# A float32 encoder trunk on one core: every operand of a matrix product begins at a multiple of 256 bytes

## The chip, the cores and the metric

The kernel runs on one core of one Trainium2 chip. The metric is the device time of one execution in microseconds (us). Before the change the median of three runs is 2270.95 us (2270.53 to 2271.29).

## The reference, cut to what matters

The reference computes a trunk of two layers over 256 tokens of width 2048, in float32. Layer 0 is a combined input projection, a bidirectional mLSTM of 4 heads and an RG-LRU block next to each other, and an output projection. Layer 1 is dilated attention of 16 heads. Each layer ends in a SwiGLU feed-forward block, and a last RMS norm stands at the end. The part of layer 0 that the change touches, and the feed-forward block in which most of the products lie:

```python
hm = bidirectional_mlstm(qh, kh, vh, gates)
hm = hm * lax.rsqrt(jnp.mean(jnp.square(hm), axis=-1, keepdims=True) + RMS_EPS)
hm = jnp.transpose(hm, (0, 2, 1, 3)).reshape(B, S, MLSTM_WIDTH) * head_g.astype(jnp.float32)
y_a = hm * jax.nn.sigmoid(o.astype(jnp.float32))
y = jnp.concatenate([y_a, y_b], axis=-1).astype(h.dtype)
return y @ w_out

def swiglu(h, w1, w3, w2):
    return (jax.nn.silu(h @ w1) * (h @ w3)) @ w2
```

## The kernel before, in words

**Products.** The kernel gets near float32 accuracy out of the fp32r type by splitting each operand into a high part (the value cast to fp32r) and a low part (the rest). A product is then three matrix products: high by high, high by low and low by high. Weights come from HBM in units of 1 MB, `raw`, of 4 blocks of 128 rows by 512 columns. `emit_split` turns half a unit at a time into `wh` (line 204, ScalarE) and `wl` (line 205, VectorE). The four `raw` buffers are loaded over SP's queue, a new one as soon as the last half of an old one is split; splits are made three steps ahead of the products (`AHEAD`).

**Two forms.** A step is one half unit. In the narrow form (`narrow`, lines 272 to 274) the activations are the stationary operand, 128 tokens at a time, and 512 weight columns move: the sums have tokens on the partitions. This form serves the value and output gates of layer 0, the attention's values, all up and down projections of the feed-forward blocks and both output projections. A step has 12 products (2 blocks of rows, 2 halves of the tokens, 3 products), a unit 24. In the wide form (lines 294 and 295) 128x128 weights are stationary and the activations move, 512 columns (high and low part of all tokens) with `wh`, then 256 with `wl`. It serves the projections whose results are wanted with features on the partitions.

**Order.** `emit_step` writes out, step by step, the splits that come next, the products of the step and then one turn of the open tasks (`run_tasks`), which are generators: evacuations of finished sums, and the recurrent parts and attention heads, of which up to three are open at once. Each engine works through its own part of this order; `flags` hold a product's instructions back until its activations have been written out.

**Where things lie.** Tiles come out of pools, and the pools stand in SBUF one behind the other, in the order in which they are opened: `const`, `rawp`, `whp`, `wlp`, `evp`, `s8p`, `m4p`, `rbp`, `smp`. Inside a pool the tiles (or the buffers of one tag) follow each other in the order of their first use, each rounded up to 32 bytes for a partition. The build places the first tile of `const` at byte 16512 of each partition. In `const` lie the constants `cpk` (gains, biases and the like, a column for each block of 128 features), `cst` (identity and two triangles), `ehr`, `gbias`, `ones`, `half`, `hgh` and then `xT`, the activations of the layer as [128, 16 blocks, high and low, 256 tokens]; small tiles of 1216 bytes in all come behind. `s8p` has eight slots of `SLOT` values each, which hold among others `hT` (the activations of the down projections), `oT` (of the attention's output projection) and `ya`/`yb` (of layer 0's output projection). `m4p` has five tiles.

**The head gain.** `more_consts` loads `head_g` into `hgh`, [128, 1024], the same row on each partition, with a DMA from POOL's queue, and halves it (line 1016). `o_chunk` computes the tanh of the gate sums (line 790) and, on line 795, (tanh + 1) times `hgh` into `go`. `ml_out` multiplies the normed heads by `go` (line 760), transposes 128x128 blocks into PSUM, and writes the high part (line 773, ScalarE, two blocks at a time) and the low part (line 774, VectorE) into `ya`.

Of the kernel before, what the change touches and what calls it, by code (L numbers as in the profile page):

```python
# [9 lines left out]
F32 = mybir.dt.float32  # L10
F32R = mybir.dt.float32r
AF = mybir.ActivationFunctionType
ALU = mybir.AluOpType
# [4 lines left out]
P = 128  # L18
KB = D // P
CW = 512  # L20
# [4 lines left out]
RB = 8  # L25
# [5 lines left out]

G_E, G_F0, G_O, G_F1 = 0, 16, 32, 48
C_W, C_B = 64, 96
C_BA, C_BX, C_LAM = 104, 120, 136
C_N = 152


RAW_BUFS = 4
# [1 line left out]
AHEAD = 3  # L40

SLOTS = 8
SLOT = 2064
EV_BUFS = 6
M4_BUFS = 5

# [18 lines left out]
def trunk_kernel(ctx: ExitStack, tc: tile.TileContext, a, out):  # L65
    nc = tc.nc
    V, A, PE, GP, SP = nc.vector, nc.scalar, nc.tensor, nc.gpsimd, nc.sync

    const = ctx.enter_context(tc.tile_pool(name="const", bufs=1))
# [5 lines left out]
    m4p = ctx.enter_context(tc.tile_pool(name="m4p", bufs=M4_BUFS))  # L75
# [7 lines left out]
    def slot(shape, dt=F32, name="s8"):  # L83
        t = s8p.tile([P, SLOT], dt, tag="s8", name=name)
        n = int(np.prod(shape))
        v = t[:, :n]
        if len(shape) == 1:
            return v
        pat = {2: "p (a b) -> p a b", 3: "p (a b c) -> p a b c", 4: "p (a b c d) -> p a b c d"}[len(shape)]
        return v.rearrange(pat, **dict(zip("abcd"[1:], shape[1:])))  # L90

    def m4(shape, name="m4", dt=F32):
        t = m4p.tile([P, 1040], dt, tag="m4", name=name)
        n = int(np.prod(shape))
        return t[:, :n].rearrange("p (a b) -> p a b", b=shape[1])

    def ev(name="ev"):
        return evp.tile([P, CW], F32, tag="ev", name=name)

    def tp(name="tp"):  # L100
        return tpp.tile([P, 2, 256], F32, tag="tp", name=name)
# [6 lines left out]
    def lag():  # L108

        for _ in range(LAG):  # L110
            yield
# [10 lines left out]
    def sm(n, name="sm"):  # L122
        t = smp.tile([P, 32], F32, tag="sm", name=name)
        return t[:, :n]

    def bcast(ap_dram, n):
        return bass.AP(tensor=ap_dram.tensor, offset=ap_dram.offset, ap=[[0, P], [1, n]])


    cpk = const.tile([P, C_N], F32, name="cpk")  # L130
    cst = const.tile([P, 3, P], F32, name="cst")
    ehr = const.tile([MH, MH, P], F32R, name="ehr")
    gbias = const.tile([P, 16], F32, name="gbias")
    ident, upper, lower = cst[:, 0, :], cst[:, 1, :], cst[:, 2, :]
    ones = const.tile([P, P], F32, name="ones")
    half = const.tile([P, 16], F32, name="half")
    hgh = const.tile([P, 1024], F32, name="hgh")
    xT = const.tile([P, KB, 2, S], F32R, name="xT")

    def transpose(o, i, n=P):  # L140
        PE.transpose(o, i, ident[:n, :n])  # L141

    def power(dst, src, n):
        GP.tensor_tensor(dst, src, half[:, :n], op=ALU.pow)
# [34 lines left out]
    pos = {"load": 0, "split": 0}  # L179
# [336 lines left out]
    ml, ys = {}, {}  # L516
# [228 lines left out]
    def ml_out(c):  # L745
        while not {f"mh{2 * c}", f"mh{2 * c + 1}", f"go{c}"} <= flags:
            yield
        rs = sm(4, "mrs").rearrange("p (a b) -> p a b", a=2)
        V.tensor_scalar(rs, ml["ss"][:, :, 2 * c:2 * c + 2], 1.0 / DV, EPS, op0=ALU.mult, op1=ALU.add)
        rsf = rs.rearrange("p a b -> p (a b)")  # L750
        power(rsf, rsf, 4)
        yield
        yt = slot((4, 2, S), F32R, name="ya")
        ys["y", 4 * c] = yt
        es = []
        for t in range(2):
            y = ev("ya")
            for k in range(2):
                h = 2 * c + k
                V.scalar_tensor_tensor(  # L760
                    y[:, k * DV:(k + 1) * DV], ml["h"][:, t, h, :], rs[:, t, k:k + 1],
                    ml["go"][:, t, h * DV:(h + 1) * DV], op0=ALU.mult, op1=ALU.mult,
                )
            es.append(y)
        yield
        yield from lag()
        for p in range(2):
            ps = tp("yT")
            for k in range(2):
                for t in range(2):  # L770
                    f0 = (2 * p + k) * P
                    transpose(ps[:, k, t * P:(t + 1) * P], es[t][:, f0:f0 + P])
            A.copy(yt[:, 2 * p:2 * p + 2, 0, :], ps)
            V.tensor_tensor(
                yt[:, 2 * p:2 * p + 2, 1, :], ps, yt[:, 2 * p:2 * p + 2, 0, :].bitcast(F32), op=ALU.subtract
            )
            for k in range(2):
                flags.add(f"y{4 * c + 2 * p + k}")
            yield

    def o_chunk(c):
        def gen(ch):
            if c == 0:
                ml["go"] = slot((2, 1024), name="go")
                ml["ro"] = const.tile([P, 2], F32, name="ro")
                V.tensor_scalar(ml["ro"], cur["rstd"], 0.5, None, op0=ALU.mult)
            es = []
            for t in range(2):
                e = ev("oe")
                A.activation(e, ch.acc[t], AF.Tanh, scale=ml["ro"][:, t:t + 1])  # L790
                es.append(e)
            ch.acc = None
            yield
            for t in range(2):
                V.scalar_tensor_tensor(
                    ml["go"][:, t, c * CW:(c + 1) * CW], es[t], 1.0, hgh[:, c * CW:(c + 1) * CW],
                    op0=ALU.add, op1=ALU.mult,
                )
            flags.add(f"go{c}")
            yield  # L800

        return gen
# [203 lines left out]
    def more_consts():  # L1006
        GP.dma_start(cst, a["cst"])
        GP.dma_start(gbias, bcast(a["gate_b"], 16))
        ehot = ev("ehot")[:MH, :]
        GP.dma_start(ehot, a["ehot"].rearrange("p a b -> p (a b)"))  # L1010
        while pos["split"] < 16:
            yield
        GP.dma_start(hgh, bcast(a["head_g"], 1024))
        while pos["split"] < 24:
            yield
        V.tensor_scalar(hgh, hgh, 0.5, None, op0=ALU.mult)
        A.copy(ehr.rearrange("p a b -> p (a b)"), ehot)

    def first_rstd():
# [96 lines left out]
    ch = steps[-1]["ch"]  # L1116
# [23 lines left out]
def tiled(w):  # L1140

    k, n = w.shape
    return np.ascontiguousarray(w.reshape(k // 512, 4, P, n // CW, CW).transpose(3, 0, 2, 1, 4))


def blocks(w):

    n = w.shape[1]
    return np.ascontiguousarray(w.reshape(KB, P, n // P, P).transpose(2, 1, 0, 3)).reshape(n // P, P, 4, CW)


def per_partition(v):
    return v.reshape(-1, P).T
# [17 lines left out]
def arrange(x, e_norm, e_w_in, e_gate_b, e_conv_w, e_conv_b, e_rg_wa, e_rg_ba, e_rg_wx, e_rg_bx,  # L1171
            e_rg_lam, e_head_g, e_w_out, o_norm, o_w_qkv, o_w_o, f_norm, f_w1, f_w3, f_w2, final_norm):
    c = np.ascontiguousarray
    w = e_w_in[0]
    q, k, v, o, g, xr, gr = np.split(w, np.cumsum([512, 512, 1024, 1024, 16, 1024])[:6], axis=1)
    perm = np.r_[0:4, 8:12, 4:8, 12:16]
    cst, ehot, ab = constants()
    cpk = np.concatenate(
        [per_partition(e_norm[0]), per_partition(f_norm[0]), per_partition(o_norm[0]), per_partition(f_norm[1]),
         e_conv_w[0].reshape(4, RB, P).transpose(2, 1, 0).reshape(P, 32), per_partition(e_conv_b[0]),  # L1180
         per_partition(e_rg_ba[0].reshape(-1)), per_partition(e_rg_bx[0].reshape(-1)),
         per_partition(e_rg_lam[0].reshape(-1))], axis=1)
    rgw = np.stack([e_rg_wa[0], e_rg_wx[0]]).reshape(2, 2, RB // 2, 2, P, P)
    return {
        "xT": c(x[0].T.reshape(KB, P, S).transpose(1, 0, 2)),
        "x": c(x[0].reshape(2, P, D).transpose(1, 0, 2)),
        "w_v": tiled(v), "w_xr": blocks(xr), "w_qk": blocks(np.concatenate([q, k], axis=1)),
        "w_og": tiled(o), "w_gr": blocks(gr),
        "wg": c(g[:, perm].reshape(KB, P, 16).transpose(1, 0, 2)),
        "gate_b": c(e_gate_b[0][perm]),  # L1190
        "head_g": c(e_head_g[0]),
        "cpk": c(cpk), "cst": cst, "ehot": ehot, "abias": ab,
        "rgw": c(rgw.transpose(2, 4, 0, 1, 3, 5)).reshape(RB // 2, P, 8, P),
        "w_out": tiled(e_w_out[0]),
        "w_av": tiled(o_w_qkv[0][:, 2 * D:]), "w_aqk": blocks(o_w_qkv[0][:, :2 * D]),
        "w_o": tiled(o_w_o[0]),
        "w1": np.stack([tiled(f_w1[l]) for l in range(2)]),
        "w3": np.stack([tiled(f_w3[l]) for l in range(2)]),
        "w2": np.stack([tiled(f_w2[l]) for l in range(2)]),
        "final_norm": c(final_norm),  # L1200
    }
# [17 lines left out]
```

## Time and profile before

| | |
|---|---|
| median of three runs | 2270.95 us |
| the profiled execution | 2270.73 us |
| its span, first to last instruction | 2269.0 us |
| TensorE busy | 2251.6 us, 99% |
| VectorE busy | 1248.0 us, 55% |
| ScalarE busy | 1042.9 us, 46% |
| granted TensorE clock | 0.999 |
| read from HBM | 414.09 MB, 183 GB/s over the span |

An instruction's row names its source line, engine, operation, the tiles that it writes and reads, shapes and count. Busy time of TensorE counts each product from its start to its modelled end; products are pipelined, so one begins before the last has ended, and the mean duration of a product is longer than the distance from its start to the next one's. That distance is read from the timeline, which lists instructions in order with start and duration.

### The profile page before, as it was taken

The page shows a single profiled execution, that of the slowest core. Times are in us where ns is not written, and L with a number is a line of the kernel's source. Part 1 is how long each engine was busy: PE and PEld are TensorE (multiplying, and loading weights), DVE is VectorE, ACT ScalarE, POOL GpSimd, SP SyncE. Part 2 cuts the span into 40 slices and gives each one's busy share as a digit, 9 for nine tenths or more (in the row PEclk, how much of TensorE's full clock was granted, in tenths as well). Part 3 has the DMA queues.
Part 4 walks back from the last instruction along what each step waited for, and adds up shares of the span by engine and source line. Part 5 has one row for each costly group of instructions (what it writes and reads, how often), then busy time and mean ns, then how long its engine had stood idle before and what let it go on. Part 6 is the DMA issues. An engine that isn't in the chain of part 4 may idle for free.

```text
span 2269.0 us, 25922 instructions
## 1 busy us (share of the span) xinstructions
PE 2251.6 (99%) x10420; PEld 1846.6 (81%) x10420; DVE 1248.0 (55%) x1514; ACT 1042.9 (46%) x1339; POOL 23.8 (1%) x42
## 2 busy tenths in 40 slices
PE   9999999999999999999999999999999999999998
PEld 7878888888888888888888888888888888888886
DVE  6867755445444444455566666554455444444554
ACT  5667544444443344444454554454444433444443
POOL 1000000000000000000000000000000000000000
PEclk9999999999999999999999999999999999999999
DMA  7534645555555555555555555555555556555553
GB/s 287 185 121 149 223 167 193 185 184 184 184 186 193 194 186 186 185 185 171 191 191 177 178 182 176 176 179 185 185 185 183 186 190 217 181 187 186 184 190 112
DMA packets 61336, 417.86 MB, mean 184 GB/s; under 512 B 6972, under 2 KB 7628, under 8 KB 12448
## 3 DMA queue, kind: packets, MB, share of 16 engines
q1 hardware_dynamic: 58176, 406.35, 52.7%
q0 software_dynamic: 2608, 9.26, 1.2%
q8 instruction: 81, 1.33, 0.2%
q10 hardware_dynamic: 432, 0.60, 0.1%
q14 instruction: 39, 0.32, 0.0%
HBM read 414.09 MB, written 2.10 MB: 183 GB/s over the span
## 4 chain that ended last, share of the span: by engine, by line
PE 95%; DVE 2%; ACT 1%; issue 1%; DMA 1%; POOL 0%; POOLq 0%; DVEq 0%; SPq 0%; ACTq 0%
PE acc L272 26%; PE acc L273 26%; PE acc L274 26%; PE acc L294 8%; PE acc L295 4%; PE hTp L141 1%; DVE wl L205 1%; PE rgp L455 1%; ACT wh L204 1%; DMA raw<-in_w_v 1%; PE nT L141 0%; DVE xc L422 0%; PE apT L141 0%; PE num L725 0%; PE asc L863 0%
## 5 line engine op out<-in xcount | busy, mean ns | idle before, releaser
L205 DVE TENSOR_TENSOR wl<-raw,wh 128x1024 fp32r<-128x1024 f32 (+1 forms) x770 | 940.3, 1222 | 876.4 <-ACT wh L204 874.3
L204 ACT CAST wh<-raw 128x1024 fp32r<-128x1024 f32 (+1 forms) x770 | 804.3, 1046 | 905.3 <-PE acc L274 828.1
L272 PE MATMUL acc<-wh,xT 128*128 128x512 f32 x1664 | 663.8, 399 | 0.9 <-ACT wh L204 0.8
L273 PE MATMUL acc<-wl,xT 128*128 128x512 f32 x1664 | 657.5, 395 | 1.2 <-DVE wl L205 1.2
L274 PE MATMUL acc<-wh,xT 128*128 128x512 f32 x1664 | 657.2, 395 | 0.0
L274 PEld LDWEIGHTS acc<-wh,xT 128*128 128x128 f32 x1664 | 312.4, 188 | 75.9
L272 PEld LDWEIGHTS acc<-wh,xT 128*128 128x128 f32 x1664 | 312.4, 188 | 75.7 <-ACT wh L204 2.0
L273 PEld LDWEIGHTS acc<-wl,xT 128*128 128x128 f32 x1664 | 312.5, 188 | 74.7 <-DVE wl L205 2.2
L294 PE MATMUL acc<-xT,wh 128*128 128x512 f32 x896 | 322.0, 400 | 0.4 <-ACT v L663 0.4
L272 PE MATMUL acc<-wh,hT 128*128 128x512 f32 x704 | 277.4, 394 | 0.0
L273 PE MATMUL acc<-wl,hT 128*128 128x512 f32 x704 | 275.9, 392 | 0.0
L274 PE MATMUL acc<-wh,hT 128*128 128x512 f32 x704 | 275.8, 392 | 0.0
L295 PE MATMUL acc<-xT,wl 128*128 128x256 f32 x896 | 252.2, 281 | 0.0
L294 PEld LDWEIGHTS acc<-xT,wh 128*128 128x128 f32 x896 | 168.5, 188 | 38.9 <-ACT v L663 0.5
L295 PEld LDWEIGHTS acc<-xT,wl 128*128 128x128 f32 x896 | 168.2, 188 | 0.9 <-DVE wl L205 0.3
L274 PEld LDWEIGHTS acc<-wh,hT 128*128 128x128 f32 x704 | 132.2, 188 | 29.8
L272 PEld LDWEIGHTS acc<-wh,hT 128*128 128x128 f32 x704 | 132.3, 188 | 28.8
L273 PEld LDWEIGHTS acc<-wl,hT 128*128 128x128 f32 x704 | 132.4, 188 | 28.6
L963 ACT CAST hT<-hTp 128x512 fp32r<-128x512 f32 x44 | 25.8, 587 | 85.2 <-PE hTp L141 85.2
L964 DVE TENSOR_TENSOR hT<-hTp,hT 128x512 fp32r<-128x512 f32 x44 | 30.4, 691 | 57.1 <-ACT hT L963 57.1
L272 PE MATMUL acc<-wh,oT 128*128 128x512 f32 x128 | 51.0, 398 | 0.0
L274 PE MATMUL acc<-wh,oT 128*128 128x512 f32 x128 | 50.3, 393 | 0.0
(226 smaller groups left out, 1209.9 us busy)
## 6 DMA issues: line engine op xcount, KB each, us to landing
raw<-in_w SPq DMA_DIRECT2D x264, 1024.0 KB, 4.9
raw<-in_w_aqk SPq DMA_DIRECT2D x32, 1024.0 KB, 4.9
raw<-in_w_out SPq DMA_DIRECT2D x16, 1024.0 KB, 4.9
raw<-in_w_av SPq DMA_DIRECT2D x16, 1024.0 KB, 4.8
raw<-in_w_o SPq DMA_DIRECT2D x16, 1024.0 KB, 4.9
raw<-in_w_xr SPq DMA_DIRECT2D x8, 1024.0 KB, 8.6
raw<-in_w_qk SPq DMA_DIRECT2D x8, 1024.0 KB, 4.9
raw<-in_w_og SPq DMA_DIRECT2D x8, 1024.0 KB, 4.9
```

Source lines behind the costliest of these rows:

```text
L141: PE.transpose(o, i, ident[:n, :n])
L204: A.copy(hi[:, k], raw[:, k])
L205: V.tensor_tensor(lo[:, k], raw[:, k], hi[:, k].bitcast(F32), op=ALU.subtract)
L272: PE.matmul(acc, xh, hi[:, j, :], start=f, stop=False)
L273: PE.matmul(acc, xh, lo[:, j, :], start=False, stop=False)
L274: PE.matmul(acc, xl, hi[:, j, :], start=False, stop=e)
L294: PE.matmul(acc, wh[:, j, :], x2.rearrange("p a b -> p (a b)"), start=f, stop=False)
L295: PE.matmul(acc[:, :S], wl[:, j, :], x2[:, 0, :], start=False, stop=e)
L455: PE.matmul(ps[:, k * S:(k + 1) * S], wt[:, k, d, b, :], xc[:, b, :], start=True, stop=True)
L963: A.copy(h[:, 2 * p:2 * p + 2, 0, :], ps)
L964: V.tensor_tensor(h[:, 2 * p:2 * p + 2, 1, :], ps, h[:, 2 * p:2 * p + 2, 0, :].bitcast(F32), op=ALU.subtract)
```

## The change: places and sizes in SBUF, and the head gain on the other side of the transposition

The constants are put into another order, `cpk` is rounded up to 192 columns and gets the head gains as eight more columns, a slot grows from 2064 to 2112 values and an m4 tile from 1040 to 1088. `hgh` becomes eight columns, a gain for each partition, halved from `cpk`; its broadcast from HBM is gone. The gate `go` is only tanh + 1, written in place. The gain is multiplied in when `ya` is written, block by block, with the scalar operand of each partition. The arithmetic of the products and their order stay as they are.

```diff
@@ constants of the file
-C_BA, C_BX, C_LAM = 104, 120, 136
-C_N = 152
+C_BA, C_BX, C_LAM, C_HG = 104, 120, 136, 152
+C_N = 160
-SLOT = 2064
+SLOT = 2112
@@ m4
-        t = m4p.tile([P, 1040], dt, tag="m4", name=name)
+        t = m4p.tile([P, 1088], dt, tag="m4", name=name)
@@ trunk_kernel, the constants
-    cpk = const.tile([P, C_N], F32, name="cpk")
+    gbias = const.tile([P, 16], F32, name="gbias")
+    half = const.tile([P, 16], F32, name="half")
+    cpk = const.tile([P, 192], F32, name="cpk")[:, :C_N]
     cst = const.tile([P, 3, P], F32, name="cst")
     ehr = const.tile([MH, MH, P], F32R, name="ehr")
-    gbias = const.tile([P, 16], F32, name="gbias")
     ident, upper, lower = cst[:, 0, :], cst[:, 1, :], cst[:, 2, :]
     ones = const.tile([P, P], F32, name="ones")
-    half = const.tile([P, 16], F32, name="half")
-    hgh = const.tile([P, 1024], F32, name="hgh")
     xT = const.tile([P, KB, 2, S], F32R, name="xT")
+    hgh = const.tile([P, 16], F32, name="hgh")[:, :RB]
@@ ml_out
-            A.copy(yt[:, 2 * p:2 * p + 2, 0, :], ps)
-            V.tensor_tensor(
-                yt[:, 2 * p:2 * p + 2, 1, :], ps, yt[:, 2 * p:2 * p + 2, 0, :].bitcast(F32), op=ALU.subtract
-            )
             for k in range(2):
+                kb = 2 * p + k
+                g = hgh[:, 4 * c + kb:4 * c + kb + 1]
+                A.mul(yt[:, kb, 0, :], ps[:, k, :], g)
+                V.scalar_tensor_tensor(
+                    yt[:, kb, 1, :], ps[:, k, :], g, yt[:, kb, 0, :].bitcast(F32), op0=ALU.mult, op1=ALU.subtract
+                )
                 flags.add(f"y{4 * c + 2 * p + k}")
@@ o_chunk
-            es = []
+            go = ml["go"][:, :, c * CW:(c + 1) * CW]
             for t in range(2):
-                e = ev("oe")
-                A.activation(e, ch.acc[t], AF.Tanh, scale=ml["ro"][:, t:t + 1])
-                es.append(e)
+                A.activation(go[:, t, :], ch.acc[t], AF.Tanh, scale=ml["ro"][:, t:t + 1])
             ch.acc = None
             yield
-            for t in range(2):
-                V.scalar_tensor_tensor(
-                    ml["go"][:, t, c * CW:(c + 1) * CW], es[t], 1.0, hgh[:, c * CW:(c + 1) * CW],
-                    op0=ALU.add, op1=ALU.mult,
-                )
+            V.tensor_scalar(go, go, 1.0, None, op0=ALU.add)
@@ more_consts
-        while pos["split"] < 16:
-            yield
-        GP.dma_start(hgh, bcast(a["head_g"], 1024))
         while pos["split"] < 24:
             yield
-        V.tensor_scalar(hgh, hgh, 0.5, None, op0=ALU.mult)
+        V.tensor_scalar(hgh, cpk[:, C_HG:C_HG + RB], 0.5, None, op0=ALU.mult)
@@ arrange: the head gains become columns of cpk
-         per_partition(e_rg_lam[0].reshape(-1))], axis=1)
+         per_partition(e_rg_lam[0].reshape(-1)), per_partition(e_head_g[0])], axis=1)
-        "head_g": c(e_head_g[0]),
```

## The prediction

> **What bounds the kernel now.** I read the page first, its busy shares and its chain.
>
> ```profile
> span 2269.0 us, 25922 instructions
> PE 2251.6 (99%) x10420; PEld 1846.6 (81%) x10420; DVE 1248.0 (55%) x1514; ACT 1042.9 (46%) x1339; POOL 23.8 (1%) x42
> PE 95%; DVE 2%; ACT 1%; issue 1%; DMA 1%; POOL 0%; POOLq 0%; DVEq 0%; SPq 0%; ACTq 0%
> PE acc L272 26%; PE acc L273 26%; PE acc L274 26%; PE acc L294 8%; PE acc L295 4%; PE hTp L141 1%; DVE wl L205 1%; PE rgp L455 1%; ACT wh L204 1%; DMA raw<-in_w_v 1%; PE nT L141 0%; DVE xc L422 0%; PE apT L141 0%; PE num L725 0%; PE asc L863 0%
> ```
>
> TensorE is busy 99% of the span and holds 95% of the chain, 90% of it in the five product lines 272 to 274, 294 and 295. So the time is their number times the distance from one start to the next (the pitch). The groups by shape give the numbers:
>
> ```profile
> L272 PE MATMUL acc<-wh,xT 128*128 128x512 f32 x1664 | 663.8, 399 | 0.9 <-ACT wh L204 0.8
> L294 PE MATMUL acc<-xT,wh 128*128 128x512 f32 x896 | 322.0, 400 | 0.4 <-ACT v L663 0.4
> L272 PE MATMUL acc<-wh,hT 128*128 128x512 f32 x704 | 277.4, 394 | 0.0
> L272 PE MATMUL acc<-wh,oT 128*128 128x512 f32 x128 | 51.0, 398 | 0.0
> L272 PE MATMUL acc<-wh,ya 128*128 128x512 f32 x64 | 25.7, 401 | 0.0
> L272 PE MATMUL acc<-wh,yb 128*128 128x512 f32 x64 | 25.2, 394 | 0.0
> ```
>
> Lines 273 and 274 have the same counts as 272, line 295 that of 294. So there are 3 x 2624 = 7872 products of 512 columns with tokens stationary (4992 with xT, 2112 with hT, 384 each with oT and y), and 896 pairs on lines 294 and 295. The mean of 399 ns is a duration that overlaps the next product; the pitch comes from the timeline.
>
> Next I set pitch against address. The build of the kernel before puts the const pool at byte 16512 = 64 x 256 + 128. By the tiles' sizes xT then begins 96 bytes past a multiple of 256, and wh and wl (the moving operand of lines 272 to 274) 32 past one. The eight slots of 8256 bytes that hold hT, oT and y begin 32, 96, 160, 224 and again 32, 96, 160, 224 past one. Call d the stationary operand's start less the moving one's, modulo 256: xT has d = 64, the slots have 0, 64, 128, 192. Steps on t, j or kb are multiples of 512 bytes and leave d alone. The second layer's down projection goes through all four, and its timeline (start, length, line) shows where one slot gives way to the next:
>
> ```profile
> 1817.43 0.39 PE L272 MATMUL acc<-wh,hT 128*128 128x512 f32 x1
> ...
> 1828.34 0.40 PE L272 MATMUL acc<-wh,hT 128*128 128x512 f32 x1
> ...
> 1833.92 0.39 PE L272 MATMUL acc<-wh,hT 128*128 128x512 f32 x1
> ...
> 1839.42 0.39 PE L272 MATMUL acc<-wh,hT 128*128 128x512 f32 x1
> ...
> 1845.01 0.39 PE L272 MATMUL acc<-wh,hT 128*128 128x512 f32 x1
> ```
>
> The first stretch is 48 products with d = 0: 10.91 us / 48 = 227.3 ns. The next three are 24 products each: d = 128, 5.58 / 24 = 232.5 ns; d = 192, 5.50 / 24 = 229.2; d = 64, 5.59 / 24 = 232.9. Same instruction, same wh and wl, one neighbourhood: the address alone moves the pitch by 2.5%. For xT, d = 64, one up-projection stretch:
>
> ```profile
> 431.90 0.48 PE L272 MATMUL acc<-wh,xT 128*128 128x512 f32 x1
> ...
> 473.98 0.49 PE L141 MATMUL hTp<-cst,up 128*128 128x128 f32 x3
> L272 PE MATMUL acc<-wh,xT 128*128 128x512 f32 x60 | 23.8, 397 | 0.0
> ```
>
> That is 180 products (60 on each line) in 42.08 us, 233.8 ns with a longer first one (0.48 against 0.39), so 233.3 as the steady value: the d = 64 value of hT again.
>
> **The change part by part.** *Addresses.* gbias and half (64 bytes each) now stand first: 16512 + 128 = 65 x 256. cpk takes 768 bytes, cst 1536, ehr 2048, ones 512, so xT begins at 21504 = 84 x 256. Behind it the shrunken hgh (64) and the small tiles (1216, as before) make 1280 = 5 x 256; raw, wh, wl and ev are multiples of 256; slots are 8448 = 33 x 256 and m4 tiles 4352 = 17 x 256. So every d becomes 0 and every start 0. That this happens I take as worked out.
>
> d = 0 is measured, but only with both operands 32 past a multiple of 256; nothing in this trace begins at 0. I price at the d = 0 row, 227.3. The bounds: above, nothing gained (pitches as now); below, the pitch of a pass without the extra time, from these pieces of the chain of waits:
>
> ```profile
> 181.12 0.86 PE qkp L682 x4
> 1125.66 0.87 PE nT L141 x8
> ```
>
> Four passes of plain float32, which take 512 columns' time each, cost 0.86 / 4 = 215 ns, and eight 128-column transpositions 0.87 / 8 = 109 ns. Products of lines 272 to 274 have 12 ns above that even at d = 0.
>
> [...]
>
> The terms for the narrow products, the units of 24 counted by the slots the build hands out (hT: 32 units at d = 0, 32 at 192, 16 at 64, 8 at 128; oT 4 at 0, 8 at 192, 4 at 64; y 4 each):
> - xT: 4992 x (233.3 - 227.3) = 30.0 us.
> - d = 64: 576 x 5.6 = 3.2 us. d = 128: 288 x 5.2 = 1.5 us. d = 192: 1056 x 1.9 = 2.0 us. d = 0: 960, nothing.
>
> *The wide pairs* (moving xT, stationary wh or wl, d = 192). A run of 56 pairs in the attention, then the scores behind it:
>
> ```profile
> 1146.42 0.40 PE L294 MATMUL acc<-xT,wh 128*128 128x512 f32 x1
> ...
> 1165.97 0.28 PE L862 MATMUL asc<-aqk 128*128 128x256 f32 x1
> ...
> 1166.68 0.39 PE L294 MATMUL acc<-xT,wh 128*128 128x512 f32 x1
> L294 PE MATMUL acc<-xT,wh 128*128 128x512 f32 x56 | 19.6, 393 | 0.0
> ```
>
> 19.55 / 56 = 349 ns a pair. The scores are six 256-column products whose two operands lie in one tile, d = 0, and take 0.71 / 6 = 118 ns each. So a pair at d = 0 is 227.3 + 118 = 345 ns: 896 x 4 = 3.6 us. Bounds: 0, and down to 215 + 109 = 324, 896 x 25 = 22.4 us.
>
> *The gate of the heads.* The gain moves from o_chunk (line 795) to the transposed side (lines 773 and 774), cut in two for a gain per partition.
>
> ```profile
> L371 ACT ACTIVATE xT<-nT,cpk 128x256 fp32r<-128x256 f32 x48 | 22.4, 473 | 29.1 <-DVE xT L372 16.4 <-PE nT L141 12.7
> L773 ACT CAST ya<-yT 128x512 fp32r<-128x512 f32 x4 | 2.3, 578 | 2.9 <-PE yT L141 2.9
> L372 DVE SCALAR_TENSOR_TENSOR xT<-nT,cpk,xT 128x256 fp32r<-128x256 f32 x48 | 22.9, 483 | 13.3 <-ACT xT L371 13.0
> L774 DVE TENSOR_TENSOR ya<-yT,ya 128x512 fp32r<-128x512 f32 x4 | 2.7, 686 | 1.9 <-ACT ya L773 1.9
> L795 DVE SCALAR_TENSOR_TENSOR go<-oe,hgh 128x512 f32<-128x512 f32 x4 | 2.6, 684 | 0.0
> L1016 DVE TENSOR_SCALAR hgh<-hgh 128x1024 f32<-128x1024 f32 x1 | 0.7, 683 | 0.0
> ```
>
> Lines 371 and 372 are the very forms that lines 773 and 774 become. ScalarE: eight of 473 for four of 578, +1.5 us. VectorE: eight of 483 for four of 686, +1.1; two additions of 128x1024 at 683 (line 1016's form) for four of 684, -1.4; hgh's own scaling shrinks by up to 0.7. Where it falls:
>
> ```profile
> 200.00:300.00 100.00, 99.98 (x501) 83.70 (x500) 72.22 (x116) 57.97 (x83) 3.49 (x4) 1.00 0.55 190
> L274 PE MATMUL acc<-wh,ya x64: 388/393/401, 282.6 to 362.9; 128*128 128x512 f32 x64
> L774 DVE TENSOR_TENSOR ya<-yT,ya x4: 682/686/691, 230.0 to 269.4; 128x512 fp32r<-128x512 f32 x4
> ```
>
> TensorE is full there (99.98 of 100), VectorE (72) and ScalarE (58) have room, and y is done at 270 us while its first product starts at 282. What queues behind the added pieces are weight splits, made three steps ahead. I count 0; uncovered it costs at most 1.5 us. The broadcast of head_g leaves POOL's queue and the DMA engines (line 1013, 128 x 1024 x 4 bytes); between -0.5 and 0, I take 0. cpk's rows grow from 608 to 640 bytes, and the first product waits for raw weights, not for cpk: 0. Transpositions and small float32 products already sit at 109 and 215 ns: 0.
>
> *Sum.* 30.0 + 3.2 + 1.5 + 2.0 + 3.6 = 40.3 us. A part of it lies before 200 us, where gaps for ScalarE and VectorE will give some back; I take off 1 us. The profiled execution took 2270.73 us (2269.0 span and 1.7 around it), and the median is 2270.95. 2270.7 - 39.3 = 2231 us, its own range 2222 to 2250 (pitches of 226 to 230 throughout).
>
> **The rivals.** *Start zero removes the extra time too.* Only distance was seen, never a start at 0. If 32 past a line costs both readers something, the narrow pitch goes from 227.3 towards 215 and the pair from 345 towards 324: 7872 x 12.3 + 896 x 21 = 116 us more, 2115 us; half of it gives 2173. For it: plain float32 passes reach 215 with a weight load each. Against: they stream at half the rate, and the scores at d = 0 give 118, not 109. [...]
>
> *The stationary operand's own start decides, and 0 is bad.* The moving operand never varies on lines 272 to 274, so d and the stationary start can't be told apart there. With starts at 32, 96, 160 and 224 giving 227.3, 232.9, 232.5 and 229.2, the neighbours of 0 are the two good ones, and their mean, 228.3, would give 7872 x 1.0 = 8 us less gain, 2239. But if reads that all begin on the same boundary meet more often, every narrow product could cost what xT's costs now, 233.3: the d = 0 products lose 960 x 6.0, d = 192 1056 x 4.1, d = 64 and 128 0.4 and 0.8 each, +10.6 us, 2281. The place is the down and output projections. It decides from a common pitch of (4992 x 233.3 + 576 x 232.9 + 288 x 232.5 + 1056 x 229.2 + 960 x 227.3) / 7872 = 232.0 ns upward.
>
> *Nothing changes.* The pitch would belong to the slot's use and not to its address: 2270.7. Against it, xT and the hT slot with d = 64 agree to 0.4 ns in different stages.
>
> **How the numbers follow.** Forecast (2222 to 2250) 0.64; start zero pays too (2115 to 2222) 0.18; a smaller gain (2250 to 2266) 0.05; no change 0.05; the bad start (2275 and up) 0.08. A measurement of this kernel can tell about 0.2%, 4.5 us, from no change. So faster is 0.64 + 0.18 + 0.05 = 0.87, same 0.05, slower 0.08. The range 2170 to 2262 holds the forecast, most of the smaller gain and about half of the lower case, 0.79.
>
> **What would show it.** Right: stretches of 180 xT products take 41.0 us instead of 42.1, all slots of hT have one pitch near 227, pairs 345, and the gaps before lines 272 to 295 stay as small as they are. Wrong: pitches that still differ by slot (address isn't it), one common pitch near 233 (start decides), near 215 (a lower cost of start zero), or new waits of line 272 for ScalarE or VectorE between 200 and 300 us.

## The result, and the profile after

The kernel after takes 2234.31 us (median of 4 runs, 2233.82 to 2234.76); the kernel before took 2270.74 us beside it. The ratio is 0.9839, with a 95% interval of 0.9822 to 0.9856: 36.4 us faster.

The page of the kernel after, its span, its busy times and the engines of its chain:

```profile
span 2233.0 us, 25927 instructions
PE 2213.9 (99%) x10420; PEld 1845.1 (83%) x10420; DVE 1247.2 (56%) x1516; ACT 1046.7 (47%) x1343; POOL 23.2 (1%) x41
...
PE 95%; DVE 2%; ACT 2%; issue 1%; DMA 0%; SPq 0%; POOL 0%; POOLq 0%; DVEq 0%; ACTq 0%
```

The number of products is the same, 10420, and TensorE is as full as before. So the products themselves got closer together. (Line numbers are one higher than before: 273 to 275 are the narrow products, 295 and 296 the wide ones.) The timeline of the kernel after, at the same place of the second down projection where four stretches were read before (the first of 48 products goes through two slots, the others through one each); start, length, line:

```profile
1790.09 0.39 PE L273 MATMUL acc<-wh,hT 128*128 128x512 f32 x1
...
1800.97 0.39 PE L273 MATMUL acc<-wh,hT 128*128 128x512 f32 x1
...
1806.41 0.39 PE L273 MATMUL acc<-wh,hT 128*128 128x512 f32 x1
...
1811.85 0.39 PE L273 MATMUL acc<-wh,hT 128*128 128x512 f32 x1
...
1817.29 0.39 PE L273 MATMUL acc<-wh,hT 128*128 128x512 f32 x1
```

48 products in 10.88 us, then three times 24 in 5.44 us: 226.7 ns in all four stretches, where there had been 227.3, 232.5, 229.2 and 232.9. Slots are now 33 x 256 bytes apart, and by the places that the build hands out the last two stretches stand at an odd multiple of 256 from the moving operand, the first two at an even one: with the same pitch, it is the remainder by 256 that counts and not the one by 512. The up-projection stretch of 180 products, with the count of one of its three lines:

```profile
428.35 0.48 PE L273 MATMUL acc<-wh,xT 128*128 128x512 f32 x1
...
469.27 0.27 PE L142 MATMUL hTp<-cst,up 128*128 128x128 f32 x1
L273 PE MATMUL acc<-wh,xT 128*128 128x512 f32 x60 | 23.4, 391 | 0.0
```

40.92 us for 180 products, 227.3 ns, against 42.08 and 233.8 before. And the run of 56 wide pairs ahead of the first attention head:

```profile
1127.82 0.39 PE L295 MATMUL acc<-xT,wh 128*128 128x512 f32 x1
...
1147.59 0.28 PE L859 MATMUL asc<-aqk 128*128 128x256 f32 x1
L295 PE MATMUL acc<-xT,wh 128*128 128x512 f32 x56 | 19.8, 399 | 0.0
```

Here it went the other way: 19.77 / 56 = 353 ns a pair, against 349 before.

For totals I took the start of every product record of both traces and summed the distances to the next start. Narrow products: 1839.6 us before, 1802.0 after, -37.6. Wide pairs: 322.9 and 325.5, +2.6. Everything else between the first and last product: 96.9 and 95.9, -1.0. Together -36.0, the difference of the spans (2269.0 and 2233.0).

What the moved head gain did shows between 200 and 300 us. The row of that stretch (busy time of TensorE first), and what TensorE waited for in it:

```profile
200.00:300.00 100.00, 98.29 (x498) 82.79 (x497) 71.44 (x118) 57.71 (x84) 3.49 (x4) 1.00 0.54 190
PE num L726 <- DVE w L712: 1.2, 1, 1.2
PE acc L296 <- DVE wl L206: 0.5, 1, 0.5
```

TensorE is busy 98.29 us of these 100, where it had been 99.98, and waits 1.2 us for a VectorE operation of a head and 0.5 us for a weight split.

### The profile page after: what moved, and what is told of

It is laid out like the page before. It is cut to its first block, busy times and chain, and to the rows that moved or that the text cites. A ratio compares the mean times of both kernels' runs of the same rounds, so it can differ in the third digit from the quotient of the medians.

```text
span 2233.0 us, 25927 instructions
## 1 busy us (share of the span) xinstructions
PE 2213.9 (99%) x10420; PEld 1845.1 (83%) x10420; DVE 1247.2 (56%) x1516; ACT 1046.7 (47%) x1343; POOL 23.2 (1%) x41
## 4 chain that ended last, share of the span: by engine, by line
PE 95%; DVE 2%; ACT 2%; issue 1%; DMA 0%; SPq 0%; POOL 0%; POOLq 0%; DVEq 0%; ACTq 0%
PE acc L273 26%; PE acc L275 26%; PE acc L274 26%; PE acc L295 9%; PE acc L296 4%; ACT wh L205 1%; DVE wl L206 1%; PE hTp L142 1%; PE rgp L456 1%; PE nT L142 0%; DMA raw<-in_w_v 0%; PE apT L142 0%; PE num L726 0%; DVE xres L346 0%; PE asc L861 0%
## 5 line engine op out<-in xcount | busy, mean ns | idle before, releaser
L273 PE MATMUL acc<-wh,xT 128*128 128x512 f32 x1664 | 654.8, 394 | 0.9 <-ACT wh L205 0.8
L274 PE MATMUL acc<-wl,xT 128*128 128x512 f32 x1664 | 648.4, 390 | 1.4 <-DVE wl L206 1.4
L275 PE MATMUL acc<-wh,xT 128*128 128x512 f32 x1664 | 648.5, 390 | 0.0
```

The lines of the kernel that those rows point to most:

```text
L273: PE.matmul(acc, xh, hi[:, j, :], start=f, stop=False)
L274: PE.matmul(acc, xh, lo[:, j, :], start=False, stop=False)
L275: PE.matmul(acc, xl, hi[:, j, :], start=False, stop=e)
```

## The experiments

Two theories were to be told apart. D: the distance d from the start of the moving operand to that of the stationary one, modulo 256 bytes, sets the pitch. S: the stationary operand's own start does. (The moving operand's own start is no third one: wh and wl began 32 past a multiple of 256 in every stretch of the kernel before, and the pitch changed all the same.) Beside them stood the question what the moved head gain did. All pitches below that are called means are taken from the starts of the records, over all products of that kind in the run's trace that are followed by another of the same form; distances of 300 ns and more (waits) are left out. The granted TensorE clock was 0.998 or 0.999 in every run, so it explains none of the differences.

**Places and gain apart.** `e_places` is the kernel before with the places alone. Since the broadcast gain stays in SBUF, m4 tiles are 4096 bytes to make room.

```diff
-SLOT = 2064
+SLOT = 2112
-        t = m4p.tile([P, 1040], dt, tag="m4", name=name)
+        t = m4p.tile([P, 1024], dt, tag="m4", name=name)
+    gbias = const.tile([P, 16], F32, name="gbias")
+    half = const.tile([P, 16], F32, name="half")
-    cpk = const.tile([P, C_N], F32, name="cpk")
+    cpk = const.tile([P, 192], F32, name="cpk")[:, :C_N]
...
     xT = const.tile([P, KB, 2, S], F32R, name="xT")
+    const.tile([P, 16], F32, name="pad")
```

> The places alone: constants reordered, cpk 192 wide, slots of 8448 bytes, m4 tiles of 4096, and a filler of 64 bytes, so that every operand begins at a multiple of 256; the head gain stays as in the kernel before. If the places are the whole cause: narrow pitch 227 ns, narrow products 37 to 38 us shorter than before, time 2232 to 2235. If the moved gain carried a part of the gain: over 2238. If the moved gain costs what its stage lost (about 1.7 us of TensorE between 200 and 300 us): 2232 to 2233.

Measured: 2233.89 us, ratio 0.9836 (0.9821 to 0.9851). The first 48 products of the same place in its timeline, and its row from 200 to 300 us:

```profile
1789.82 0.39 PE L273 MATMUL acc<-wh,hT 128*128 128x512 f32 x1
...
1800.70 0.39 PE L273 MATMUL acc<-wh,hT 128*128 128x512 f32 x1
200.00:300.00 100.00, 99.63 (x505) 84.15 (x504) 73.19 (x117) 57.45 (x82) 3.49 (x4) 1.00 0.54 190
```

48 products in 10.88 us, and 99.63 us of 100 busy. The narrow products take 1801.6 us in all, 38 less than before. The places are the whole gain.

`e_gain` is the kernel after with the old sizes and the old order of the constants, and a filler that puts xT, wh, wl and the slots back where they were.

```diff
-SLOT = 2112
+SLOT = 2064
-        t = m4p.tile([P, 1088], dt, tag="m4", name=name)
+        t = m4p.tile([P, 1040], dt, tag="m4", name=name)
...
+    const.tile([P, 1000], F32, name="pad")
     xT = const.tile([P, KB, 2, S], F32R, name="xT")
```

> The moved head gain alone: order of constants, slot and m4 sizes as before, with a filler so that xT, wh, wl and the slots begin where they began (96, 32, 32 and 32/96/160/224 past a multiple of 256). If the places are the whole cause: narrow pitch 233 ns for xT, time 2270 to 2273, the upper end if the moved gain causes the gaps near 240 us. If the moved gain helps by itself: under 2268.

Measured: 2272.12 us, ratio 1.0004 (0.9995 to 1.0013). Its timeline over two of the four stretches and its one wait of TensorE between 200 and 300 us:

```profile
1819.41 0.39 PE L274 MATMUL acc<-wh,hT 128*128 128x512 f32 x1
...
1830.31 0.40 PE L274 MATMUL acc<-wh,hT 128*128 128x512 f32 x1
...
1835.89 0.39 PE L274 MATMUL acc<-wh,hT 128*128 128x512 f32 x1
PE num L727 <- DVE w L713: 1.2, 1, 1.2
```

The pitches are those of before, 10.90 / 48 = 227.1 and 5.58 / 24 = 232.5 ns. The wait of 1.2 us is there with the moved gain and without the places, and is absent from `e_places`. In the time this is 1 us that can't be told from nothing.

**Distance or start.** `e_start96` moves everything of the kernel after on by 96 bytes, where xT had stood before.

```diff
+    const.tile([P, 24], F32, name="pad")
     gbias = const.tile([P, 16], F32, name="gbias")
```

> The kernel after with a filler of 96 bytes ahead of all constants: every operand begins 96 past a multiple of 256, the distance d stays 0. If the distance decides: narrow pitch 227 ns, time 2232 to 2237. If the stationary operand's own start decides: narrow pitch 233 ns as for xT before, 7872 x 6 = 47 us more, 2281. If a multiple of 64 is worth something beside the distance: in between.

Measured: 2235.00 us, ratio 0.9840 (0.9825 to 0.9854).

```profile
1790.25 0.39 PE L274 MATMUL acc<-wh,hT 128*128 128x512 f32 x1
...
1801.13 0.39 PE L274 MATMUL acc<-wh,hT 128*128 128x512 f32 x1
```

10.88 us again, 226.7 ns. No operand of the five product lines begins at a multiple of 256 or even of 64, and nothing is lost. S falls.

`e_n64` leaves the stationary operands at multiples of 256 and moves wh and wl on by 192 bytes, in narrow steps alone, so d = 64. Its edit is the frame of all later ones: the split buffers get 256 bytes more, and the part that is used begins at an offset (in values of 4 bytes) chosen by the form of the step.

```diff
-        hi = whp.tile([P, 2, CW], F32R, tag="wh", name="wh")
-        lo = wlp.tile([P, 2, CW], F32R, tag="wl", name="wl")
+        oh, ol = (0, 0) if st["wide"] else (48, 48)
+        hi = whp.tile([P, 2 * CW + 64], F32R, tag="wh", name="wh")[:, oh:oh + 2 * CW].rearrange("p (a b) -> p a b", b=CW)
+        lo = wlp.tile([P, 2 * CW + 64], F32R, tag="wl", name="wl")[:, ol:ol + 2 * CW].rearrange("p (a b) -> p a b", b=CW)
```

> The kernel after with wh and wl 192 bytes further on in the narrow steps alone: all starts are still multiples of 64, xT and the slots begin at 0, and d is 64. If the distance decides: narrow pitch 233 ns, wide pairs as in the kernel after, time 2234 + 7872 x 6 = 2281. If the stationary operand's own start decides: narrow pitch 227, time 2234.

Measured: 2281.87 us, ratio 1.0048 (1.0031 to 1.0065), slower than the kernel before.

```profile
1824.55 0.39 PE L274 MATMUL acc<-wh,hT 128*128 128x512 f32 x1
...
1835.75 0.39 PE L274 MATMUL acc<-wh,hT 128*128 128x512 f32 x1
```

11.20 / 48 = 233.3 ns. The narrow products take 1848.6 us, 46.6 more than in the kernel after. The stationary side stands where it stood, and 192 bytes on the moving side cost the whole gain and more (before, a part of the slots had better distances). The longer buffers alone are not the cause: in `e_w64` below, which has them too and leaves narrow steps at d = 0, the narrow products take 1800.5 us. D holds, to the microsecond that it forecast.

**Other distances.** `e_d224` and `e_d32` put wh and wl 32 and 224 bytes further on in all steps.

```diff
+        oh, ol = (8, 8) if st["wide"] else (8, 8)      # e_d224
+        oh, ol = (56, 56) if st["wide"] else (56, 56)    # e_d32
```

> The kernel after with wh and wl 32 bytes further on in all steps: narrow d = 224, wide d = 32. If the cost goes in steps of 64 bytes: narrow pitch 227 (as d = 0) or 229 (as d = 192), time 2234 to 2252. If it goes smoothly with d: between the two, 228 ns, time 2242. If a start off a multiple of 64 lets the two reads miss each other altogether: pitch near 216, under 2160.

> The kernel after with wh and wl 224 bytes further on in all steps: narrow d = 32, wide d = 224. If the cost goes in steps of 64 bytes: narrow pitch 227 (as d = 0) or 233 (as d = 64), time 2234 or 2281. If smoothly: 230 ns, time 2258.

Measured: `e_d224` 2281.52 us, ratio 1.0047 (1.0030 to 1.0064); `e_d32` 2277.20 us, ratio 1.0029 (1.0018 to 1.0040). The timeline of `e_d224`:

```profile
1824.77 0.40 PE L274 MATMUL acc<-wh,hT 128*128 128x512 f32 x1
...
1835.97 0.40 PE L274 MATMUL acc<-wh,hT 128*128 128x512 f32 x1
```

And of `e_d32`:

```profile
1820.79 0.40 PE L274 MATMUL acc<-wh,hT 128*128 128x512 f32 x1
...
1831.99 0.40 PE L274 MATMUL acc<-wh,hT 128*128 128x512 f32 x1
```

Both 11.20 / 48 = 233.3 ns. The cost neither goes smoothly with d, nor in steps of 64 bytes to both sides of 0: 32 bytes off in either direction is as bad as 64. Of the 4.3 us between the two runs 3.9 come from the wide pairs (325.0 and 321.1 us in all; more below).

Finer and further distances, with wh and wl apart:

```diff
+        oh, ol = (60, 4) if st["wide"] else (60, 4)     # e_d16_240
+        oh, ol = (40, 24) if st["wide"] else (40, 24)    # e_d96_160
```

> The same look at d = 16 (narrow products with wh, moved on by 240 bytes) and d = 240 (those with wl, moved on by 16). If 227 needs the very same place: 233 ns for both, time 2281. If it needs a distance under 32: 227 for both, time 2234.

> One look at two more distances in one kernel: wh 160 bytes and wl 96 bytes further on in all steps, so the narrow products with wh have d = 96 and those with wl d = 160; the wide products have d = 160 for wh and 96 for wl. If all distances but 0 (and partly 192) are slow: narrow pitches 233 ns, time 2281. If the cost dips at other distances: 227 to 230 for one of them.

Measured: 2291.61 and 2283.12 us, one run each. The timeline of `e_d16_240`:

```profile
1830.73 0.40 PE L274 MATMUL acc<-wh,hT 128*128 128x512 f32 x1
...
1842.04 0.40 PE L274 MATMUL acc<-wh,hT 128*128 128x512 f32 x1
```

11.31 / 48 = 235.6 ns, the worst of all. The means over the traces, narrow products (xT stationary, with wh and with wl moving; where the two have different d, the one that has it; in the kernel before the slots hT, oT and y, within one slot):

| d, bytes | mean pitch, ns | from |
|---|---|---|
| 0 | 227.3 and 227.0 (wh and wl moving) | after |
| 16 | 234.8 | e_d16_240, wh |
| 32 | 233.2 and 233.3 | e_d32 |
| 64 | 233.3 and 233.3 | e_n64 |
| 96 | 232.8 | e_d96_160, wh |
| 128 | 232.8 and 232.7 | before, slots |
| 160 | 234.4 | e_d96_160, wl |
| 192 | 229.4 and 229.7 | before, slots |
| 224 | 233.3 and 233.2 | e_d224 |
| 240 | 236.0 | e_d16_240, wl |

The rows for 16, 96, 160 and 240 are mixtures. In these two runs a product's neighbours have another distance than its own, and it shows: the first and the third of the three product lines both move wh at one d, and with xT stationary take 235.6 and 233.8 ns at d = 16 and 233.6 and 232.1 at d = 96. Where all of them have one d, these two lines differ by 0.3 ns at most. So the neighbour's distance counts too, and no run has 16, 96, 160 or 240 throughout.

**The wide pairs.** `e_w64` and `e_w128` move wh and wl on in wide steps alone.

```diff
+        oh, ol = (16, 16) if st["wide"] else (0, 0)    # e_w64
+        oh, ol = (32, 32) if st["wide"] else (0, 0)    # e_w128
```

> The kernel after with wh and wl 64 bytes further on in the wide steps alone; narrow steps keep d = 0, the wide ones go from d = 0 to d = 64. The kernel after has 235.4 + 117.0 = 352.4 ns a pair there, the kernel before (d = 192) 232.5 + 119.3 = 351.7. If the wide pairs follow the same rule as the narrow products (0 best, 64 worst): pair over 356, time 2237 to 2240. If a pair is bound by its two weight loads whatever the address: pair 351 to 353, time 2234.

> The kernel after with wh and wl 128 bytes further on in the wide steps alone, so d = 128 there. Same rule as narrow: pair over 356 ns, 2237 to 2240. Bound by its loads whatever the address: pair 351 to 353, 2234. A rule of its own: any other pair, 0.9 us for each ns.

Measured: 2235.40 us (ratio 0.9845, 0.9830 to 0.9859) and 2234.08 us (0.9838, 0.9823 to 0.9853). The means of a pair, first and second product: d = 0 235.4 + 117.0 = 352.4 ns (after); 64, 234.7 + 118.6 = 353.3; 128, 230.6 + 120.4 = 351.0; 192, 232.5 + 119.3 = 351.7 (before); `e_d224`, whose wide pairs had d = 32, gave 352.3. So the narrow rule is not theirs, and these five lie within 2.3 ns. But `e_d32`, whose wide pairs had d = 224, gave 228.9 + 118.5 = 347.4. Alone in `e_best`:

```diff
+        oh, ol = (56, 56) if st["wide"] else (0, 0)    # e_best
```

> The kernel after with wh and wl 224 bytes further on in the wide steps alone: narrow d = 0 (227 ns a product), wide d = 224 (229 + 118.5 = 347.4 ns a pair instead of 352.4). If each form has its own best distance and the two add up: 896 x 5 = 4.5 us under the kernel after, 2230. If the wide steps' gain at d = 224 hung on the narrow steps being shifted too: 2234.

Measured: 2230.81 us (5 runs, 2230.40 to 2231.32), ratio 0.9824 (0.9810 to 0.9837). The 56 pairs of the attention in its timeline:

```profile
1127.41 0.39 PE L296 MATMUL acc<-xT,wh 128*128 128x512 f32 x1
...
1146.83 0.28 PE L860 MATMUL asc<-aqk 128*128 128x256 f32 x1
```

19.42 / 56 = 346.8 ns a pair against 353 in the kernel after; over the whole trace 347.4 against 352.4, with narrow products at 227. By the pitches that is 4.5 us; by the medians it is 3.5 us under the kernel after, though the two were not timed on one chip side by side and their intervals overlap. It is the fastest version seen, level with the next.

The last run asked whether each wide product has its own distance, that to the weights loaded while it runs (in the trace of the kernel after a wide product of 512 columns and the load of the wl behind it both start at 1128.51 us; the load takes 0.19 us). In `e_d16_240` the second product, with wl at d = 16 and the next wh at d = 240, had taken only 113.9 ns (the first took 233.1, so that pair, 346.9, was no better than the one at 224).

```diff
+        oh, ol = (60, 56) if st["wide"] else (0, 0)    # e_best2
```

> The kernel after with wh 240 and wl 224 bytes further on in the wide steps alone. What the earlier runs gave by itself: a 512-column product whose next weights are wl at d = 224 takes 228.9 ns, a 256-column one whose next weights are wh at d = 240 takes 113.9. If the pitch is set by the distance from the moving operand to the weights that are loaded meanwhile: 342.8 ns a pair, 896 x 4.6 = 4.1 us under the kernel with 224 for both, 2226 to 2228. If it is set by the product's own weights, or by both: 347 ns or more, 2231.

Measured: 2230.81 us (5 runs), ratio 0.9825 (0.9811 to 0.9838). A miss: 229.4 + 118.0 = 347.3 ns a pair. The next wh stands at d = 240 as in `e_d16_240`, and the second product does not keep the 113.9 ns. Nor is it each product's own weights: the first has wh at d = 240 in both runs and takes 233.1 and 229.4 ns. So the two distances don't act one by one. How they act together stays open.

## Why the prediction was right, step by step

The forecast was 2231 us, with 2222 to 2250 as its own range; measured 2234.31. The likeliest mechanism was the right one. The number is near because the narrow products are nine tenths of the sum; of the small terms two were wrong, and it is luck that they came to no more than a few microseconds.

**What bounds, and pitch against address.** Confirmed. The reading of one stretch of the kernel before, where the slots changed under the same instruction, held for the whole kernel. That it is distance and not start, which that trace could not show, `e_start96` and `e_n64` show.

**The narrow products, 36.7 us.** Measured 37.6 (1839.6 to 1802.0 us), 38.0 in `e_places`. The price of d = 0 was taken from operands 32 past a multiple of 256, 227.3 ns; at 0 it is 227.2.

**The wide pairs, 3.6 us.** This term had the wrong sign: nothing was saved, and the pairs themselves got 0.6 us longer (351.7 to 352.4 ns each; in `e_places` the total is 323.5 us against 322.9). The step that failed is "a pair at d = 0 is 227.3 + 118 = 345 ns". It carried the rule of the narrow products over to a form in which a long and a short product alternate. At d = 0 the first product of a pair takes 235.4 ns, more than the 232.5 it had at d = 192, and the second 117.0 instead of 119.3. The base, 349 ns, was also read from one good run of pairs; the mean of the trace was 351.7. The other 2.0 us of the +2.6 in the total are two waits that fall behind wide products, and belong to the next term.

**The gate of the heads, 0, and 1.5 us if uncovered.** The cover failed: TensorE waits 1.2 us near 240 us in the kernel after and in `e_gain`, not in `e_places`, and in the kernel after 0.5 us for a weight split. Together that is 1.7 us of idle time (2.0 in distances from start to start), just over the 1.5 given as the most. In the time it doesn't show: the kernel after and `e_places` are 0.4 us apart (2234.31 and 2233.89), and outside the five product lines the kernel after is 2.1 us shorter than `e_places`; what gave that back is open. The prediction looked at when y is needed (it is needed later) and at weight splits. It didn't look at the head's own VectorE work, which stands behind the pieces of y in VectorE's order. The pieces in the trace of the kernel after show why they are longer than their sum: line 778's halves on VectorE wait for line 777's on ScalarE, and the other way round.

```profile
231.19 0.47 ACT L777 ACTIVATE ya<-yT,hgh 128x256 fp32r<-128x256 f32 x1 [1.32 <-DVE ya L778]
231.70 0.48 DVE L778 SCALAR_TENSOR_TENSOR ya<-yT,hgh,ya 128x256 fp32r<-128x256 f32 x1 [0.54 <-ACT ya L777]
```

**The sum.** Span against span, 39.3 us were forecast and 36.0 came. The wide pairs fell short by 4.2 and the gate added 2.0; the narrow products gave 0.9 more, and everything outside the five lines gave 1.0 where 1.0 had been taken off.

**The rivals.** "Start zero removes the extra time too" fell: 227 ns at start 0, at 32 (before) and at 96 (`e_start96`). "The stationary operand's own start decides" fell with the same run and with `e_n64`; but the price given for it, 2281, is what a bad distance costs (2281.87 in `e_n64`). "Nothing changes" rested on the pitch not belonging to the address, and fell with `e_places`. The narrow products took 227 ns in the kernel after and 233 in `e_n64`, where wh and wl alone are moved by 192 bytes. Why the distance costs time, and whether it has to do with reads that meet, no run here shows.

The remaining 12 ns over the 215 of a plain float32 pass (line 682 of the kernel before, 0.86 us for four) were at no distance removed; what they are is open. So is why d = 192 gave 229 ns in most stretches of the kernel before. That such a pass takes the time of 512 columns, and so bounds a narrow product, was the author's estimate: the kernel before shows 215 ns for a pass of 256 columns (`128x256`), 118 for a score product of 256 and 227.3 for a narrow product of 512 at d = 0.

## What to carry to other kernels

Where a product of fp32r operands is bound by TensorE, look at the distance from start to start before trusting that it has no slack, and compare stretches in which only a buffer changes: two buffers with different pitches under one instruction (227.3 and 232.5 ns in the kernel before) pointed to the address here. Put both operands of a narrow product at the same place modulo 256 bytes; where that place itself lies was worth nothing here (226.7 ns a product at 0 and at 96), and a shift of 32 bytes on one side alone lost 2% (`e_d224` against the kernel after, 2281.52 and 2234.31 us). Try each form of product by itself: what was best for 512 columns alone, d = 0, was not for the pairs of 512 and 256 (352.4 ns there, 347.4 at d = 224).

## What the runs showed of the hardware that I had not expected

Among the distances tried the good one is a point and not a region. At d = 0 a 512-column fp32r product follows the last after 227 ns; at 16 bytes off it takes 234.8 (d = 16) and 236.0 ns (d = 240), worse than at 32 or 64 off (233.3), though these two were seen only next to each other in one run. The neighbours at 32 and 224 that I would have drawn a smooth curve through, 228 to 230 ns, are as slow as the far ones (233.2 to 233.3 ns at 32 and 224, 233.3 at 64). For pairs of 512 and 256 columns the best single distance found was 224 (347.4 ns), exactly where the narrow products are slow (233.3 and 233.2 ns).
